# Eight pairs' channel transforms: the low parts of the left operands against the table's high half only

## The chip, the cores and the metric

The kernel runs on one core of a Trainium2 chip. The metric is the device time of one execution in microseconds (us); for the kernel before it is 1575.81 us, the median of three runs (1575.69 to 1577.49). One execution was profiled.

## The reference

Two layers work on a prompt of 2048 positions and a sample of 512, each of width 1024, in float32. Layer 0 is windowed attention. Layer 1, in which the change lies, mixes by a two-dimensional Fourier transform over the positions and over the channels of each of four groups of 256:

```python
def fourier_layer(x, g, w_gate, w_out):
    b, s, d = x.shape
    h = rmsnorm(x, g)
    hg = h.astype(jnp.float32).reshape(b, s, N_FGROUPS, FGROUP_CH)
    f = jnp.fft.fftn(hg, axes=(1, 3), norm="ortho").real
    f = f.reshape(b, s, d).astype(x.dtype)
    gate = h @ w_gate
    return x + (f * jax.nn.silu(gate)) @ w_out

def trunk(x, ...):
    for i in range(DEPTH):
        j = i // N_MIXERS
        if i % N_MIXERS == 0:
            x = attention_layer(x, attn_norm[j], attn_w_in[j], attn_w_out[j], attn_sink[j], rel_bias)
        else:
            x = fourier_layer(x, fourier_norm[j], fourier_w_gate[j], fourier_w_out[j])
    return rmsnorm(x, final_norm)
```

Weights and activations are float32. Both the prompt and the sample go through the same `trunk`.

## The kernel before

**Numbers in two parts.** TensorE (PE) multiplies operands of type F32R, a float32 with fewer bits of mantissa. To come near float32, an operand is split: ScalarE (ACT) copies it into F32R, which gives the high part, and VectorE (DVE) subtracts that from the source, which gives the low part. A product of two split operands is then a sum of products of parts. `matmul3` (line 117 of the kernel) makes three of the four: high by high, high by low, low by high. Each is one load of the left operand (128 partitions by 128 columns) into the array and one matmul that streams the right operand past it, up to 512 columns, into an accumulator in PSUM.

**Stages.** The attention layer takes about the first 1060 us. From there the Fourier layer walks over ten pairs of 128-row tiles of positions: pairs 0 and 1 of the sample, then pairs 2 to 9 of the prompt. For each pair it normalises the two tiles, transposes them on PE (`turn`, line 1089, into PSUM tiles `tr...`), forms sums and differences of them, splits these (`parts`, `odd`, `cross`; lines 1013 and 1015 in `split`, lines 1096 and 1097 in `own`), and uses them twice: as left operands of the gate's products with the weights (`gates`, accumulators W, Z and X, through line 117), and as left operands of the channel transform (`z`, `z_odd_even`). A radix-4 step on DVE (`combine`, lines 1268 and 1277) then joins two pairs, and the results go to DRAM. After about 1300 us the transform over the positions and the output products follow.

**The channel transform.** `z_odd_even(i)` handles tile i of a pair: for each of four channel groups it takes a PSUM bank, and for two left operands (`odd` = 0 and 1) it multiplies by a table of 128 columns for each. The table `ch` holds its high and its low half side by side, so `ch[:, 0, :, odd * P : (odd + 1) * P]` has 2 x 128 = 256 columns. Both parts of the left operand meet both halves, which makes four products of parts in two matmuls of 256 columns (line 1160). The left operands are `S[1]` and `diff` (the trace's names `S` and `tTd`) for tile 1, and `S[4]` and `mixed` (`S` and `tC`) for tile 0. Behind the four matmuls of a group, ACT (line 1167) takes the sums that came from the table's low half out of the bank, and DVE (line 1168) adds those from its high half. The transform of tile 1 runs from hook 5 of the gate products of the pair ahead, that of tile 0 from hook 6. In pairs 0 and 1, those of the sample, tile 0 goes through `z` with `matmul3`; only their tile 1 goes through `z_odd_even`.

**What sets the order.** A planner takes the instructions as the program issues them, keeps dependencies, and sets an order for each engine by its own costs; on the chip each engine then works its list in that order and waits by semaphores. PSUM banks for the transposes and the transforms come from one pool of five, those of W, Z and X from another of three.

Of the kernel before, what the change touches and what calls it, by code (L numbers as in the profile page):

```python
# [19 lines left out]
P = 128  # L20
# [22 lines left out]
def encoder(  # L43
# [22 lines left out]
    odd = dram.tile([3, 2, P, D], F32, name="odd")  # L66
# [9 lines left out]
    def bank(name):  # L76
        if turning:
            return two_banks(name)[:, 0]
        return banks[-1].tile([P, 512], F32, tag="bank", name=name)
# [911 lines left out]
    def fourier_phase(tail):  # L991
        with ExitStack() as es:
# [13 lines left out]
            ch = ready["chan"]  # L1006

            def zt(name):
                return right([P, D], F32, name)
# [58 lines left out]
            class Pair:  # L1068
# [80 lines left out]
                def z_odd_even(self, i=1):  # L1149

                    t = self.ts[i]
                    out_of = (self.S[1], self.diff) if i else (self.S[4], self.mixed)
                    self.zs[i] = zt(f"z{t}")
                    for g in range(4):
                        ps = bank(f"z{t}_{g}")
                        for odd, m in enumerate(out_of):

                            to = ps[:, odd * 256 : odd * 256 + 256].rearrange("p (a n) -> p a n", a=2)
                            for part in range(2):
                                PE.matmul(  # L1160
                                    to, m[part][:, g * P : (g + 1) * P], ch[:, 0, :, odd * P : (odd + 1) * P],
                                    start=part == 0, stop=part == 1,
                                )
                        v = ps.rearrange("p (o a n) -> p a o n", o=2, a=2)
                        out = self.zs[i][:, g * 256 : g * 256 + 256].rearrange("p (n o) -> p o n", o=2)
                        scale = 1.0 if t >= SEQ // P else 0.5
                        ACT.activation(out, v[:, 1], AF.Copy, scale=scale)
                        last_z[0] = DVE.scalar_tensor_tensor(out, v[:, 0], scale, out, ALU.mult, ALU.add)
# [138 lines left out]
            for i, s in enumerate(tail):  # L1307
# [7 lines left out]
                if 1 <= i < 9:  # L1315
                    w, k = split_steps[i - 1]
# [690 lines left out]
```

## Time and profile before

| what | value |
|---|---|
| median of three runs | 1575.81 us (1575.69 to 1577.49) |
| the profiled execution's own time | 1575.53 us |
| its span, first to last instruction | 1573.5 us |
| mean granted TensorE clock | 0.999 |
| DVE busy | 1169.3 us (74%) |
| ACT busy | 884.9 us (56%) |
| POOL busy | 446.3 us (28%) |

The page of the profile gives the busy time of each engine, the span in 40 slices, the chain of work that ended last, and the costliest groups of instructions. PEld is the loading of left operands into the array, which has a lane of its own beside PE. A group's row reads: line, engine, operation, out <- in, the left operand's size (128*128), the size streamed, the count, busy time in us, the mean duration of one in ns, and the idle time before. The duration of a matmul includes the way through the array, so consecutive matmuls overlap: what one costs in a row of many is the distance from one start to the next, which the chain of waits shows (time over count). All F32R operands stand as "f32" in the rows.

### The profile page before, as it was taken

To read this page: it belongs to the slowest core of one execution; us is meant where nothing else is said; L and a number is where in the kernel's file an instruction comes from. 1 tells how busy PE (TensorE), PEld (TensorE's weight loads), DVE (VectorE), ACT (ScalarE), POOL (GpSimd) and SP (SyncE) were. 2 spreads that over 40 slices of the span, in tenths; PEclk is the share of its full clock that TensorE was granted. 3 is DMA by queue.
4 is the path that set the end of the run, shared out by engine and by line. 5 is a ranking of instruction groups with operands and counts; after the bars stand their busy time and mean duration, and the time that the engine had idled before them with its cause. 6 is when DMAs were issued, how large, how long until landed. Compare 5 with 4: busy or idle time off the path is not lost.

```text
span 1573.5 us, 27706 instructions
## 1 busy us (share of the span) xinstructions
PE 1561.3 (99%) x9818; PEld 1308.6 (83%) x9818; DVE 1169.3 (74%) x2841; ACT 884.9 (56%) x2120; POOL 446.3 (28%) x614
## 2 busy tenths in 40 slices
PE   9999999999999999999999999999999999999998
PEld 7888888888898888988888888888888888888886
DVE  5888665877548776377863577768989888989886
ACT  6788535677237774266851567646655564343353
POOL 2575652421403414124223142122121121111100
PEclk9999999999999999999999999999999999999999
DMA  8598695665865576656649665665565569557852
GB/s 290 196 331 292 230 360 208 222 238 201 294 228 197 203 267 234 242 193 237 256 150 330 229 232 195 245 250 205 211 238 199 207 235 409 182 201 285 296 195 94
DMA packets 100998, 373.91 MB, mean 238 GB/s; under 512 B 11267, under 2 KB 22283, under 8 KB 83452
## 3 DMA queue, kind: packets, MB, share of 16 engines
q1 hardware_dynamic: 83148, 298.17, 53.3%
q0 software_dynamic: 16400, 70.04, 11.4%
q10 hardware_dynamic: 1312, 3.94, 0.6%
q8 instruction: 78, 1.28, 0.3%
q14 instruction: 60, 0.49, 0.1%
HBM read 280.84 MB, written 91.26 MB: 236 GB/s over the span
## 4 chain that ended last, share of the span: by engine, by line
PE 89%; DMA 4%; DVE 3%; issue 2%; ACT 1%; POOL 0%; POOLq 0%; ACTq 0%; SPq 0%; DVEq 0%
PE gp L117 14%; PE qp L117 14%; PE spt L117 11%; PE op L117 7%; PE av L615 6%; PE spt L530 6%; PE W L117 5%; PE vp L117 3%; PE fo L117 3%; PE pt L589 3%; PE Wo L117 3%; PE Z L117 3%; PE z L1160 2%; PE Zo L117 2%; PE X L117 1%
## 5 line engine op out<-in xcount | busy, mean ns | idle before, releaser
L117 PE MATMUL gp<-h,wg 128*128 128x512 f32 x960 | 237.6, 396 | 0.0
L117 PE MATMUL qp<-h,wq 128*128 128x512 f32 x960 | 237.0, 396 | 0.0
L549 DVE CUSTOM_DVE_ANT_0 S<-spt,b 128x385 f32<-128x385 f32 (+1 forms) x320 | 156.5, 527 | 105.4 <-PE spt L530 68.3
L117 PEld LDWEIGHTS gp<-h,wg 128*128 128x128 f32 x960 | 174.9, 188 | 37.2 <-issue 1.0
L117 PEld LDWEIGHTS qp<-h,wq 128*128 128x128 f32 x960 | 174.9, 188 | 36.4 <-issue 0.2
L557 ACT ACTIVATE S<-S 128x385 f32<-128x385 f32 (+1 forms) x320 | 188.8, 596 | 19.5 <-DVE S L549 19.3
L597 ACT CAST pts<-pt 128x384 fp32r<-128x384 f32 (+1 forms) x240 | 100.6, 458 | 168.8 <-PE pt L589 160.1
L598 DVE TENSOR_TENSOR pts<-pt,pts 128x384 fp32r<-128x384 f32 (+1 forms) x240 | 114.3, 520 | 23.4 <-ACT pts L597 22.4
L639 POOL TENSOR_TENSOR uT<-o,uT 128x256 fp32r<-128x256 f32 x75 | 55.6, 741 | 229.4 <-ACT uT L638 229.3
L117 PE MATMUL spt<-wo,uT 128*128 128x512 f32 x480 | 120.4, 391 | 0.0
L117 PE MATMUL op<-wo,uT 128*128 128x512 f32 x480 | 118.9, 391 | 0.0
L530 PE MATMUL spt<-kwin,qab 64*128 64x384 f32 (+1 forms) x960 | 118.6, 353 | 0.0
L615 PEld LDWEIGHTS av<-pts,v 128*128 128x128 f32 x576 | 101.4, 188 | 18.8
L117 PE MATMUL fo<-wo,tTu 128*128 128x512 f32 x480 | 115.6, 392 | 0.2 <-ACT wo L1743 0.2
L615 PE MATMUL av<-pts,v 128*128 128x512 f32 (+1 forms) x576 | 115.7, 341 | 0.0
L117 PEld LDWEIGHTS op<-wo,uT 128*128 128x128 f32 x480 | 89.4, 188 | 18.5
L117 PEld LDWEIGHTS spt<-wo,uT 128*128 128x128 f32 x480 | 89.1, 188 | 18.3
L117 PEld LDWEIGHTS fo<-wo,tTu 128*128 128x128 f32 x480 | 88.2, 188 | 17.9 <-ACT wo L1743 0.6
L569 DVE TENSOR_SCALAR S<-S 128x384 f32<-128x384 f32 (+1 forms) x192 | 95.9, 499 | 6.8
L530 PEld LDWEIGHTS spt<-kwin,qab 64*128 64x128 f32 x960 | 74.6, 186 | 28.3 <-issue 25.7
L635 POOL TENSOR_TENSOR o<-o,s 128x256 f32<-128x256 f32 x75 | 55.4, 738 | 134.8 <-DVE o L633 134.5
L589 PEld LDWEIGHTS pt<-ident,S 64*128 64x128 f32 x1328 | 78.2, 138 | 4.5 <-issue 2.1
(337 smaller groups left out, 3210.6 us busy)
## 6 DMA issues: line engine op xcount, KB each, us to landing
wo<-wsd SPq DMA_DIRECT2D x32, 1024.0 KB, 5.7
wq<-wsd SPq DMA_DIRECT2D x31, 1024.0 KB, 7.3
wg<-wsd SPq DMA_DIRECT2D x31, 1024.0 KB, 5.8
x<-x1d SPq DMA_DIRECT2D x40, 512.0 KB, 3.7
b<-b21d SPq DMA_DIRECT2D x40, 512.0 KB, 4.7
b<-rowd SPq DMA_DIRECT2D x40, 384.0 KB, 4.1
xs<-in_x_dram SPq DMA_DIRECT2D x23, 512.0 KB, 7.4
s2d<-gt POOLq DMA_DIRECT2D x40, 256.0 KB, 4.2
```

The costliest lines, as they stand in the source:

```text
L117: ins = pe(PE.matmul(out, a[i], b[j], start=start and i + j == 0, stop=stop and i == 1, skip_group_check=more))
L530: pe(PE.matmul(banks[j][:, 2 + k0 * P : 2 + k1 * P], res["q"][rows, qp, b * P : (b + 1) * P], kwin[g][rows, kp, b * P + k0 * P : b * P + k ...
L549: seq(DVE, DVE.tensor_tensor_reduce(out=s[:, e0:e1], in0=ps[:, 1 + e0 : 1 + e1], in1=st["bias"][:, j, 386 - e1 : 386 - e0][:, ::-1], scale ...
L557: last_exp[0] = seq(ACT, ACT.activation(s[:, e0:e1], s[:, e0:e1], AF.Exp, bias=s[:, 386:387], scale=-1.0, accum_out=s[:, 387:388]))
L569: seq(DVE, DVE.tensor_scalar(s[:, ks], s[:, ks], den, None, ALU.mult))
L589: pe(PE.transpose(ps[h][:, kb, j, :], ss[j][rows, 1 + kb * P : 1 + (kb + 1) * P], ident[rows, rows]))
L597: seq(ACT, ACT.copy(hi, ps[:, k0:k1]))
L598: seq(DVE, DVE.tensor_tensor(lo, ps[:, k0:k1], f32(hi), ALU.subtract))
L615: pe(PE.matmul(to, v, pt, start=n == part == 0, stop=part == 1 and n in (1, len(todo) - 1), skip_group_check=n > 1,))
L635: eng.tensor_tensor(o, o, s, ALU.mult)
L639: low = eng.tensor_tensor(lo, o, f32(hi), ALU.subtract)
L1160: PE.matmul(to, m[part][:, g * P : (g + 1) * P], ch[:, 0, :, odd * P : (odd + 1) * P], start=part == 0, stop=part == 1,)
```

## The change

In `z_odd_even` the second matmul, that of the low part of the left operand (`part` = 1), takes only the high half of the table for the pairs of the prompt (`self.n > 1`): 128 columns in place of 256, and it adds to the first 128 of the 256 sums alone. The product of low part by low half is no longer made. The number of matmuls and of loads stays.

```diff
                             for part in range(2):
+                                w = 1 if part and self.n > 1 else 2
                                 PE.matmul(
-                                    to, m[part][:, g * P : (g + 1) * P], ch[:, 0, :, odd * P : (odd + 1) * P],
+                                    to[:, :w], m[part][:, g * P : (g + 1) * P], ch[:, 0, :w, odd * P : (odd + 1) * P],
                                     start=part == 0, stop=part == 1,
                                 )
```

The planner's order moves at four places on PE, and around them on the other engines. The first place is the transform of tile 0 of pair 2 (left operands S and tC), on PE, where the first product of the next gate (W, left operand tTb) is near. Before:

```order
L1160 MATMUL z_0_13359<-chan_sb,S_2_13269 128x256 x2
L1160 MATMUL z_0_13359<-chan_sb,tC_13300 128x256
L117 MATMUL W_13405<-wB_0_12646,tTb_0_13227 128x512 x2
L1160 MATMUL z_0_13359<-chan_sb,tC_13300 128x256
L117 MATMUL W_13405<-wB_0_12646,tTb_0_13227 128x512
L117 MATMUL W_13405<-wB_1_12664,tTb_0_13227 128x512
L1160 MATMUL z_1_13366<-chan_sb,S_2_13269 128x256 x2
L1160 MATMUL z_1_13366<-chan_sb,tC_13300 128x256 x2
L117 MATMUL W_13405<-wB_1_12664,tTb_0_13227 128x512 x2
L1160 MATMUL z_2_13373<-chan_sb,S_2_13269 128x256 x2
```

Now, from the end of the first group (the rows ahead of these alternate in the same way):

```order
L1161 MATMUL z_0_13359<-chan_sb,tC_13300 128x256
L1161 MATMUL z_0_13359<-chan_sb,tC_13300 128x128
L1161 MATMUL z_1_13366<-chan_sb,S_2_13269 128x256
L1161 MATMUL z_1_13366<-chan_sb,S_2_13269 128x128
L1161 MATMUL z_1_13366<-chan_sb,tC_13300 128x256
L1161 MATMUL z_1_13366<-chan_sb,tC_13300 128x128
L1161 MATMUL z_2_13373<-chan_sb,S_2_13269 128x256
L1161 MATMUL z_2_13373<-chan_sb,S_2_13269 128x128
L1161 MATMUL z_2_13373<-chan_sb,tC_13300 128x256
L1161 MATMUL z_2_13373<-chan_sb,tC_13300 128x128
```

Every second matmul is now 128 columns wide, and the six matmuls of W that stood between those of z now stand behind the last group. The same happens at tile 0 of pairs 4, 6 and 8, where seven matmuls of W move; the order of PE is otherwise as it was.

The second place is DVE just ahead of the same transform: the low part of tC (line 1015) and the addition for the first group of tile 1's transform (z_0_13314). Before:

```order
L1015 TENSOR_TENSOR S_2_13296<-s_2_13242,S_2_13296 128x512
L1243 TENSOR_TENSOR c_13156<-c_13156,X_13155 128x512
L1015 TENSOR_TENSOR tC_13300<-s_2_13242,tC_13300 128x512
L1168 SCALAR_TENSOR_TENSOR z_13313<-z_0_13314,z_13313 128x2x128
L1205 SCALAR_TENSOR_TENSOR gt_0_13309<-gt_0_13309,c_13156 128x512
```

Now:

```order
L1015 TENSOR_TENSOR S_2_13296<-s_2_13242,S_2_13296 128x512
L1244 TENSOR_TENSOR c_13156<-c_13156,X_13155 128x512
L1169 SCALAR_TENSOR_TENSOR z_13313<-z_0_13314,z_13313 128x2x128
L1015 TENSOR_TENSOR tC_13300<-s_2_13242,tC_13300 128x512
L1206 SCALAR_TENSOR_TENSOR gt_0_13309<-gt_0_13309,c_13156 128x512
```

The low part of tC, for which PE's second matmul by tC waits, now stands behind one more operation. The same two operations change places at pairs 4, 6 and 8. On ACT some operations of lines 1167, 1204, 1013 and 1056 change places with a neighbour in the same stretch, on POOL one small operation at three places, and one load of `b` on SP's queue moves ahead of two loads of `wo` near the end of the stretch.

## The prediction

> **What bounds the kernel now.** I read the page's busy times and its chain of waits first, and then the stage of the change by itself.
>
> ```profile
> span 1573.5 us, 27706 instructions
> PE 1561.3 (99%) x9818; PEld 1308.6 (83%) x9818; DVE 1169.3 (74%) x2841; ACT 884.9 (56%) x2120; POOL 446.3 (28%) x614
> PEclk9999999999999999999999999999999999999999
> PE 89%; DMA 4%; DVE 3%; issue 2%; ACT 1%; POOL 0%; POOLq 0%; ACTq 0%; SPq 0%; DVEq 0%
> ```
>
> PE is busy 99% of the span, at the full granted clock in every slice, and 89% of the chain that ended last is PE. The changed pairs run from 1108 to 1300 us; over windows the columns are the window, its length, then busy time (count) of PE, PEld, DVE, ACT and POOL, the granted clock, and the share and rate of the DMA.
>
> ```profile
> 1108.00:1300.00 192.00, 191.41 (x1018) 163.79 (x1017) 173.09 (x290) 115.15 (x234) 36.98 (x61) 1.00 0.61 217
> ```
>
> Of 192.0 us PE idles 0.6. So what a matmul of this stage costs more or less on PE, the kernel gains or loses almost in full; DVE (173.1 us, 90%) is next.
>
> **How many, and at what price now.** The groups by form in that window:
>
> ```profile
> L117 PE MATMUL W<-wT,S 128*128 128x512 f32 x184 | 45.0, 393 | 0.0
> L1160 PE MATMUL z<-chan_sb,S 128*128 128x256 f32 x128 | 25.6, 282 | 0.0
> L1089 PE MATMUL trb<-ident,x 128*128 128x128 f32 x112 | 14.5, 272 | 0.6 <-DVE x L1081 0.6
> L1160 PE MATMUL z<-chan_sb,tC 128*128 128x256 f32 x64 | 13.8, 287 | 0.0
> L1160 PE MATMUL z<-chan_sb,tTd 128*128 128x256 f32 x64 | 12.9, 283 | 0.0
> ```
>
> Line 1160 has 128 + 64 + 64 = 256 matmuls here. Every second one is of a low part: 8 pairs x 2 tiles x 4 groups x 2 operands = 128 change. Durations of about 282 ns overlap; the distance between starts stands in the chain of waits inside the window (start, length, what, count):
>
> ```profile
> 1112.09 1.91 PE z L1160 x16
> 1114.01 2.75 PE W L117 x12
> ...
> 1125.28 0.87 PE trb L1089 x8
> 1126.16 2.74 PE W L117 x12
> ```
>
> 1.91 / 16 = 119 ns for 256 columns, 2.74 / 12 = 228 ns for 512 columns, and 0.87 / 8 = 109 ns for a float32 transpose of 128 columns. From 256 to 512 columns a column costs (228 - 119) / 256 = 0.43 ns; in a transpose it costs 109 / 128 = 0.85 ns.
>
> **Term 1: the 128 narrow matmuls.** No row of this trace has a product of F32R parts under 256 columns. Some of the narrowest products and of the 128-wide transposes of the whole program:
>
> ```profile
> L117 PE MATMUL vp<-wv,h 128*128 128x256 f32 x384 | 50.3, 283 | 0.0
> L530 PE MATMUL spt<-kwin,qab 64*128 64x256 f32 x192 | 20.1, 313 | 0.0
> L117 PE MATMUL ABp<-gp,tbp 128*128 128x256 f32 x96 | 14.3, 281 | 0.0
> L1025 PE MATMUL tru<-ident,us 128*128 128x128 f32 x32 | 4.3, 273 | 0.0
> L222 PE MATMUL spt<-ident,inv 128*128 128x128 f32 x23 | 3.3, 272 | 0.0
> ```
>
> So the price of the new form has to be bounded. Below: the straight line through 512 and 256 columns, continued to 128, gives 119 - 128 x 0.43 = 64 ns. That is 55 ns less, and 128 x 55 = 7.0 us gained. Above: what is read at one column in 0.43 ns is shown for F32R from 256 columns up only; 4-byte data at 128 columns is shown only in transposes, and there a column takes twice as long, though the right operand has the same 4 bytes. If the narrow form loses the fast price of F32R and is computed as full float32, a transpose is the cheapest example of it: with the identity on one side, only one operand has two halves, and it costs 2 column times. With two such operands it is 2 x 2 = 4 column times: 128 x 4 x 0.43 = 218 ns, or, with the fixed part in the row of 512 columns, 228 ns. That is 228 - 119 = 109 ns more for each, and 128 x 109 = 14.0 us lost.
>
> The Trainium skill, page "FP8 and Floating Point Precision", section "TensorE Precision Notes", says that true float32 takes four passes through the array and that reduced precision reads float32 cut shorter. No run here shows a float32 product that isn't a transpose; by that rule, if the narrow form counts as true float32, the loss is the same 14 us.
>
> Between the two ends stands the load of the left operand, one for each matmul, whatever its width. Two windows, the first in the transform, the second in a product of 512 columns, and three groups of loads of the whole program:
>
> ```profile
> 1112.10:1113.70 1.60, 1.60 (x15) 1.60 (x15) 1.60 (x4) 1.37 (x4) 0.00 (x0) 1.00 0.59 172
> 1109.00:1111.40 2.40, 2.40 (x12) 2.01 (x11) 2.40 (x5) 0.83 (x2) 0.00 (x0) 1.00 0.75 288
> ...
> L117 PEld LDWEIGHTS W<-wT,S 128*128 128x128 f32 x240 | 44.2, 188 | 8.8 <-DVE wT L1015 0.2
> L1089 PEld LDWEIGHTS trb<-ident,x 128*128 128x128 f32 x160 | 18.5, 140 | 4.0 <-PE Z L117 1.0 <-DVE xrl L701 0.6 <-issue 0.2
> L1160 PEld LDWEIGHTS z<-chan_sb,tTd 128*128 128x128 f32 x80 | 12.6, 191 | 0.1
> ```
>
> At 256 columns PEld is busy 1.60 of 1.60 us with loads of 191 ns that overlap; at 512 columns it rests. The load already fills the time of a 256-column matmul, so the lower end of 64 ns is hardly to be reached: the narrower matmul would wait for its load. That leaves "no change" and "slower", and of these I take the upper end, 14.0 us: the only 128-wide rows of 4-byte data pay the double price per column, which says that the fast price hangs on the form and is not a property of 4-byte operands.
>
> **Term 2: the moved W products and tC.** At tile 0 of pairs 2, 4, 6 and 8, W no longer fills the time until tC's low part is there. Timeline of the first place, before:
>
> ```profile
> 1116.42 0.68 DVE L1243 TENSOR_TENSOR c<-c,X 128x512 f32<-128x512 f32 x1
> 1116.59 0.40 PE L1160 MATMUL z<-chan_sb,S 128*128 128x256 f32 x2
> 1116.97 0.39 PE L1160 MATMUL z<-chan_sb,tC 128*128 128x256 f32 x1
> 1117.02 0.68 DVE L1015 TENSOR_TENSOR tC<-s,tC 128x512 fp32r<-128x512 f32 x1
> 1117.19 0.63 PE L117 MATMUL W<-wB,tTb 128*128 128x512 f32 x2
> 1117.62 0.41 DVE L1168 SCALAR_TENSOR_TENSOR z<-z,z 128x256 f32<-128x256 f32 x1
> 1117.76 0.39 PE L1160 MATMUL z<-chan_sb,tC 128*128 128x256 f32 x1
> ```
>
> tC's low part is ready at 1117.02 + 0.68 = 1117.70, and one operation of 0.41 us now stands ahead of it: 1118.11. PE reaches the transform later by the eight narrow matmuls of tile 1 (8 x 0.109 = 0.87): 1116.59 + 0.87 = 1117.46, and the matmul by tC's low part three matmuls on (0.12 + 0.23 + 0.12): 1117.93. It waits 0.2 us at each of four places, 0.8 in all; behind it in PE's list stand the rest of z and then W. If the narrow matmuls cost no more than now, it waits 1118.11 - 1116.59 - 3 x 0.12 = 1.2 us, 4.6 us in all.
>
> Against that, a slower PE swallows waits that it has now:
>
> ```profile
> PE trb L1089 <- DVE x L1081: 0.6, 1, 0.6
> PEld z L1160 <- DVE tC L1015: 0.4, 1, 0.4
> PEld z L1160 <- ACT tC L1013: 0.2, 1, 0.2
> ```
>
> These sum to 1.2 us. I set term 2 to zero, with ends of +0.8 and -1.2 in the slow case. The four evacuations of a group and the operations that changed places on ACT, POOL and SP run beside PE and have, if PE is slower, more time than now (ACT 115.2 of 192 us); without that cover each evacuation on DVE would cost its 0.41 us.
>
> **Sum.** 1575.5 (the profiled execution's own time, 0.3 below the median of the runs) + 14.0 + 0 = 1589.5 us. This case's own ends are 128 x (218 - 119) = 12.7, less 1.2, and 128 x (240 - 119) = 15.5, plus 0.8, which gives 1587 to 1592; 240 is two pipelined loads of 119 to 120 for one matmul.
>
> **The rivals.**
>
> *The narrow form pays more still.* If a full float32 product needs its left operand loaded in two halves, and these don't overlap with the stream, a matmul costs up to 2 x 191 = 382 ns: 128 x (382 - 119) = 33.7 us, 1609. Half way, at 300 ns, it is 23.2 us, 1598.7. For it: loads already fill PEld at 256 columns. Against it: loads of 191 ns follow at 119 ns there, so they do overlap.
>
> *It takes as long as before.* The load sets the pace, 119 ns, or two column times as in a transpose, 109 ns: 0 to -1.3 us. For it: PEld without a gap. Against it: it holds only if the fast price of F32R lasts at 128 columns, or a product goes as a transpose. Term 2 then adds up to 4.6 us, less what W's later place gives back; I count 1575 to 1578, the same within what can be told.
>
> *Faster: the stream sets the pace.* One mechanism: PE takes 0.43 ns a column at 128 columns too, and the loads pipeline closer than 119 ns. It decides as soon as a matmul costs less than 119 - 3.2 / 128 x 1000 = 94 ns; at 64 ns it is -7.0 us, 1568.5, and DVE's 173.1 us would still fit into 185. For it: the straight line through two widths. Against it: PEld, which shows no shorter distance. The Trainium skill, page "TensorE: Matmul & The Clock Gate", section "Back-to-back issue gap", gives 81 ns for a load and a matmul of 128 columns and 131 ns at 512; by that it would be 128 x (119 - 81) = 4.9 us faster. The trace does not agree with it for this type: 228 ns at 512.
>
> **How the numbers follow.** About 0.2% (3.2 us) is what a measurement of this kernel can tell from no change. Forecast (1587 to 1592): 0.68. Dearer still (1592 to 1609): 0.15. As long as before: 0.09. Faster: 0.08. So slower 0.83, same 0.09, faster 0.08. The range of 1584 to 1605 holds the forecast, with 3 us below it for waits that I don't see, and most of the dearer case, about 0.8; the two other cases are left out.
>
> **What would show it.** In the profile after, a row of line 1161 with 128x128 x128 in place of half of the 256-wide ones. If I am right, its matmuls last about 390 ns (as the 393 of 512 columns) and not under 282, 16 matmuls of tile 1 take 8 x 0.12 + 8 x 0.23 = 2.8 us in the chain of waits where they take 1.91, and the stage is 206 us long where it is 192. PE stays without gaps at tile 0 of the four pairs but for some 0.2 us each. The prediction is wrong if the narrow matmuls follow one another at 119 ns or less.

## The result and the profile after

The changed kernel takes 1580.95 us (median of 6 runs, 1580.0 to 1582.39) against 1575.06 us before: ratio 1.0034, interval 1.0024 to 1.0044. In a second set on another occasion the ratio was 1.0030 (1.0019 to 1.0041). It is slower by 4 to 6 us; 14 were forecast, and the time lies below the range.

The page of the profile after, the same rows as before:

```profile
span 1577.9 us, 27706 instructions
PE 1562.3 (99%) x9818; PEld 1308.8 (83%) x9818; DVE 1169.2 (74%) x2841; ACT 884.2 (56%) x2120; POOL 442.4 (28%) x614
PE 87%; DVE 6%; DMA 3%; issue 2%; ACT 1%; POOL 0%; SPq 0%; ACTq 0%; POOLq 0%; DVEq 0%
```

The span grew by 4.4 us, while PE's busy time grew by 1.0 and the share of DVE in the chain rose from 3% to 6%. So most of the time isn't in the matmuls. Their groups by form, in a window (1099 to 1310 us) around the changed pairs:

```profile
L1161 PE MATMUL z<-chan_sb,S 128*128 128x256 f32 x64 | 20.7, 323 | 1.1 <-DVE z L1169 1.1
L1161 PE MATMUL z<-chan_sb,S 128*128 128x128 f32 x64 | 14.3, 223 | 0.0
L1161 PE MATMUL z<-chan_sb,tC 128*128 128x256 f32 x32 | 10.9, 341 | 2.6 <-ACT tC L1013 2.5
L1161 PE MATMUL z<-chan_sb,tTd 128*128 128x256 f32 x32 | 10.7, 336 | 0.0
L1161 PE MATMUL z<-chan_sb,tC 128*128 128x128 f32 x32 | 7.6, 236 | 1.6 <-DVE tC L1015 1.6
L1161 PE MATMUL z<-chan_sb,tTd 128*128 128x128 f32 x32 | 7.1, 222 | 0.0
```

The 128-wide matmuls last 222 ns, 60 less than the 282 that a 256-wide one took before, and not 390 as forecast. The end of a matmul is modelled in the profile, its start is not, and the starts say the same: the next matmul starts 0.06 us after a narrow one (timeline).

```profile
1189.38 0.22 PE L1161 MATMUL z<-chan_sb,S 128*128 128x128 f32 x1
1189.44 0.39 PE L1161 MATMUL z<-chan_sb,tTd 128*128 128x256 f32 x2
```

But the 256-wide ones now last 336 ns even where PE waits for no other engine: what one gives, the next takes. A whole transform shows the balance (chain of waits, start, length, what):

```profile
1189.43 1.79 PE z L1161 x16
1191.22 2.81 PE W L117 x12
1194.03 1.79 PE z L1161 x16
1195.82 2.81 PE W L117 x12
```

Before, 16 matmuls took 1.91 us and the twelve of W behind them 2.75; now it is 1.79 and 2.81. Together that is 4.60 where it was 4.66: some 0.07 us for each of 16 transforms, 1.1 us in all, and no more.

The loss stands in the waits of the weight loads between 1100 and 1300 us (us in total, times, longest):

```profile
PEld z L1161 <- ACT tC L1013: 3.1, 4, 1.3
PEld z L1161 <- DVE tC L1015: 2.4, 4, 0.7
PEld z L1161 <- DVE z L1169: 1.7, 4, 0.5
PEld W L117 <- DVE c L1240: 0.9, 3, 0.4
```

8.1 us in all, where the rows before had 0.6 for tC. All but the last stand at tile 0 of pairs 2, 4, 6 and 8, from where the planner had moved W away. The timeline at pair 6, rows of PE, ACT and DVE:

```profile
1218.74 0.34 PE L1161 MATMUL z<-chan_sb,S 128*128 128x256 f32 x2
1219.24 0.60 ACT L1013 CAST tC<-s 128x512 fp32r<-128x512 f32 x1
1219.36 0.42 DVE L1169 SCALAR_TENSOR_TENSOR z<-z,z 128x256 f32<-128x256 f32 x1
1219.88 0.69 DVE L1015 TENSOR_TENSOR tC<-s,tC 128x512 fp32r<-128x512 f32 x1
1219.89 0.39 PE L1161 MATMUL z<-chan_sb,tC 128*128 128x256 f32 x1 [0.81 <-ACT tC L1013]
1220.62 0.33 PE L1161 MATMUL z<-chan_sb,tC 128*128 128x128 f32 x1 [0.34 <-DVE tC L1015]
1221.28 1.08 DVE L1169 SCALAR_TENSOR_TENSOR z<-z,z 128x256 f32<-128x256 f32 x3
1221.76 0.45 PE L1161 MATMUL z<-chan_sb,S 128*128 128x256 f32 x2 [0.34 <-DVE z L1169]
```

PE waits three times in a row: for tC's high part from ACT, for its low part from DVE, and then for a bank of PSUM, which comes free when DVE has taken tile 1's transform out of it. With W between, PE had work there. The same place before:

```profile
1215.58 0.60 ACT L1013 CAST tC<-s 128x512 fp32r<-128x512 f32 x1
1215.90 0.40 PE L1160 MATMUL z<-chan_sb,S 128*128 128x256 f32 x2
1216.23 0.38 PE L1160 MATMUL z<-chan_sb,tC 128*128 128x256 f32 x1
```

The cast that makes tC's high part ended 0.3 us after the start of the transform (1216.18 against 1215.90); now it ends 1.1 us after it (1219.84 against 1218.74).

In this execution the stretch from pair 2's tile 1 (start 1111.93 before, 1110.23 after) to pair 9's tile 0 (1291.05 and 1297.68) is 8.3 us longer. The terms found come to 8.0: 8.1 of waits less the 0.6 of before, plus 1.6 of a stretch in which the clock fell to half (experiment 8), less the 1.1 gained. The span grew by 4.4 alone, since this execution was 1.7 us ahead at the start of the stretch, 1.4 of them since the first 43 us, which the change doesn't touch, and 2.2 us came back behind it, most of them where PE waits for DVE at the transform over the positions. Of the weight loads' waits from 1300 us on, before:

```profile
PEld ABp L117 <- DVE gp L1424: 3.2, 6, 0.7
PEld Bs L117 <- DVE us L1468: 1.0, 1, 1.0
```

and after:

```profile
PEld ABp L117 <- DVE gp L1425: 2.3, 5, 0.7
```

### The profile page after: what moved, and what is told of

It is laid out like the page before. It is cut to its first block, busy times and chain, and to the rows that moved or that the text cites. A ratio compares the mean times of both kernels' runs of the same rounds, so it can differ in the third digit from the quotient of the medians.

```text
span 1577.9 us, 27706 instructions
## 1 busy us (share of the span) xinstructions
PE 1562.3 (99%) x9818; PEld 1308.8 (83%) x9818; DVE 1169.2 (74%) x2841; ACT 884.2 (56%) x2120; POOL 442.4 (28%) x614
## 4 chain that ended last, share of the span: by engine, by line
PE 87%; DVE 6%; DMA 3%; issue 2%; ACT 1%; POOL 0%; SPq 0%; ACTq 0%; POOLq 0%; DVEq 0%
PE gp L117 14%; PE qp L117 14%; PE spt L117 11%; PE op L117 7%; PE av L615 6%; PE spt L530 6%; PE W L117 5%; PE fo L117 5%; PE vp L117 3%; PE pt L589 3%; PE Wo L117 3%; PE Z L117 3%; PE Zo L117 2%; PE X L117 1%; PE z L1161 1%
```

## The experiments

Two theories at the outset: A, the moved order costs the time and the narrow form nothing; B, the narrow matmuls cost it. To tell them apart, the order of the instructions was held by edges that fix only the order on an engine and add no wait, at the end of the program:

```diff
     fourier_phase(attention_phase())
+    held = (
+        [13361, 13362, 13409, 13410, 13363, 13411, 13412, 13367, ...],
+        ...
+    )
+    known = {i.name: i for i in nc.cur_bb.bb.instructions}
+    for row in held:
+        for a, b in zip(row, row[1:]):
+            tc.add_manual_dep(known[f"I-{b}"], f"I-{a}", ISSUE, reason="issue order")
```

Each row lists instructions of one engine in the order wanted. From the Fourier layer's stretch on, the orders named below hold exactly on all five engines.

**1. Narrow matmuls, old order.** The changed kernel with the rows of the kernel before.

> The changed kernel's narrow matmuls, but every engine held to the order that the kernel before has (order edges alone, no waits). Theory A, the moved order costs the time and a narrow matmul costs no more than a wide one: 16 transforms each 0.12 us shorter (1.79 us where 1.91 were, in the two traces), so about 1.9 us faster than before, 1573 us, with no wait for tC beyond that of before. Theory B, the narrow matmuls cost the time: as slow as the changed kernel, 1580 to 1581 us.

Measured: 1574.23 us against 1575.32, ratio 0.9996 (0.9987 to 1.0004). The waits of its weight loads for tC are those of before:

```profile
PEld trb L1089 <- PE Z L117: 2.3, 2, 1.3
PEld z L1161 <- DVE tC L1015: 0.4, 1, 0.4
PEld z L1161 <- ACT tC L1013: 0.3, 1, 0.3
```

B falls: the narrow form costs nothing. Its gain of about a microsecond can't be told from no change here: the interval holds 1.

**2. Wide matmuls, new order.** The kernel before with the rows of the changed one.

> The kernel before with its 256-column matmuls, every engine held to the order of the changed kernel. Theory A: nearly as slow as the changed kernel, 5 to 8 us over before (the waits at tC come back, the 1.9 us of the narrower matmuls are missing), 1580 to 1583 us. Theory B: no slower than before, 1575 us.

Measured: 1579.54 us, ratio 1.0029 (1.0018 to 1.0040), just under the range expected. A holds: the order alone makes the loss. The waits are those of the changed kernel:

```profile
PEld z L1160 <- ACT tC L1013: 3.1, 4, 1.0
PEld z L1160 <- DVE tC L1015: 2.4, 4, 0.7
PEld z L1160 <- DVE z L1168: 1.6, 4, 0.5
PEld W L117 <- DVE c L1239: 0.8, 3, 0.5
```

**3. and 4. Which part of the order.** Narrow matmuls, with PE in the old order and the other engines in the new one, and the reverse.

> The narrow matmuls, PE held to the order of before (W's products again between those of z), the other engines to the order of the changed kernel (tC's low part one operation later on DVE). Theory A1, the missing W products are what lets the waits through: near the kernel before, 1573 to 1576 us. Theory A2, the later tC on ACT and DVE is what PE waits for, and W only hides part of it: 1577 to 1579 us. Theory B: 1580 us.

> The narrow matmuls, PE held to the order of the changed kernel (W behind z), the other engines to the order of before (tC's low part one operation earlier). Theory A1: as slow as the changed kernel less 4 x 0.4 us, 1578 to 1580 us. Theory A2: most of the loss is gone, 1575 to 1577 us. Theory B: 1580 us.

Measured: 1575.5 us (1.0001, 0.9992 to 1.0010) with PE in the old order, 1579.87 us (1.0023, 1.0015 to 1.0032) with PE in the new one. So it is PE's order, W among z or behind it, that decides the time (A1). The other engines' order shows in the waits. With PE in the old order and the rest in the new one, PE still waits for tC's high part, while W covers the rest:

```profile
PEld z L1161 <- ACT tC L1013: 3.5, 4, 1.3
PEld z L1161 <- DVE tC L1015: 0.4, 1, 0.4
```

With PE in the new order and the rest in the old one, that wait is small and the two others are there:

```profile
PEld z L1161 <- DVE tC L1015: 2.1, 4, 0.6
PEld z L1161 <- DVE z L1169: 1.6, 4, 0.4
PEld z L1161 <- ACT tC L1013: 0.8, 2, 0.6
```

So the wait for the high part comes with the other engines' new order, and those for the low part and the bank with PE's. The first is hardly to be seen in the time: 1575.5 us against 1574.23 in experiment 1. In the profile of experiment 3 the stretch from pair 2's tile 1 (1110.37) to pair 9's tile 0 (1292.76) is 3.3 us longer than before, and as in the changed kernel 2.2 us come back behind it. The loss of experiment 4 doesn't look like waits alone: nine of its eleven executions had a mean granted clock of 0.997 or 0.998 and took 1578.1 to 1581.3 us, and the two with 0.999 took 1575.8 and 1575.9. How much of it is the clock's was not separated (experiment 8 has more on this).

**5. and 6. tC earlier.** If tC is what PE waits for, making it sooner should help. At the four places, the cast of tC goes ahead of the square of the next tile on ACT, and its low part directly behind that of S on DVE, once with PE in the new order and once with all else in the old one.

```diff
 DVE, at pair 2
  L1015 S_2_13296
+ L1015 tC_13300
  L1244 c_13156
  L1169 z_13313<-z_0_13314
- L1015 tC_13300
```

> The changed kernel, its PE order kept (W behind z), but at the four places tC's high part stands one operation earlier on ACT (ahead of the square of the next tile) and its low part two operations earlier on DVE. If what PE waits for is tC, and the moved W only uncovers that wait, the 8 us of waits in the stage shrink by half or more: 1574 to 1577 us. If the order of W costs by itself (bank or weight load), it stays at 1579 to 1581 us.

> The narrow matmuls in the order of the kernel before, with tC earlier in the same way. If the theory of waits is right, there is little left to gain here, 0.3 us at each of four places, set against a later square of the next tile: 1572 to 1575 us, the best of all, or equal to the kernel before.

Measured: 1583.81 us (1.0052, 1.0038 to 1.0066) in the new order, against 1574.19 us (0.9997, 0.9988 to 1.0006) in the old one. The first is a clear miss: not better but slower than the changed kernel (1578.98 us on the same occasion). Its waits:

```profile
PEld z L1161 <- DVE z L1169: 6.4, 8, 0.9
PEld z L1161 <- DVE tC L1015: 1.7, 4, 0.5
```

The wait for ACT is gone, but the wait for a bank grew from 1.7 to 6.4 us: the first of DVE's additions that free the banks now stands behind tC. The waits sum to 8.5 us with 0.4 at W, about as many as the 8.1 of the changed kernel. So tC alone is not what is short. DVE has both to do, tC's low part and the additions of tile 1, before PE can go through tile 0, and in each order of DVE's list that was tried PE lacked other work meanwhile. That this version is slower than the changed one is explained in part: its profile has a stretch at half the granted clock, worth 1.6 us, which that of the changed kernel on the same occasion hasn't (experiment 8), and it was 2.0 us behind that one already at the start of the stretch (1111.97 against 1110.02). Nor does the planner's swap of the two operations on DVE, which the prediction booked as a loss, matter much: behind PE's new order the waits for the low part and the bank are 2.1 and 1.6 us without it (experiment 4) and 2.4 and 1.7 with it.

**7. What sets the pace.** All the prompt's transform matmuls narrow, in the old order; high by high and low by high go into the two halves of the bank. This version leaves out the product of the high part with the table's low half.

```diff
-                                w = 1 if part and self.n > 1 else 2
+                                w = slice(part, part + 1) if self.n > 1 else slice(0, 2)
                                 PE.matmul(
-                                    to[:, :w], m[part][:, g * P : (g + 1) * P], ch[:, 0, :w, odd * P : (odd + 1) * P],
-                                    start=part == 0, stop=part == 1,
+                                    to[:, w], m[part][:, g * P : (g + 1) * P],
+                                    ch[:, 0, 0:1 if self.n > 1 else 2, odd * P : (odd + 1) * P],
+                                    start=part == 0 or self.n > 1, stop=part == 1 or self.n > 1,
                                 )
```

> All 256 matmuls of the prompt's transforms 128 columns wide (high by high and low by high, into the two halves of the bank; the product of the high part with the table's low half is left out), in the order of the kernel before. If the load of the left operand sets the pace (108 to 116 ns from load to load), 16 matmuls still take 1.74 to 1.8 us and the time is that of the narrow kernel in the old order, 1573 to 1575 us. If the stream sets it (60 ns after a narrow matmul), 16 take 0.96 us and the time falls by about 13 us, to 1562. If a narrow matmul were priced as full float32 (228 ns), it would rise by 28 us.

Measured: 1573.42 us, ratio 0.9988 (0.9979 to 0.9997). A transform in the chain of waits:

```profile
1187.33 1.74 PE z L1161 x16
1189.07 2.85 PE W L117 x12
```

and a window inside one (columns as before):

```profile
1111.50:1112.90 1.40, 1.40 (x15) 1.40 (x14) 1.40 (x3) 0.89 (x3) 0.00 (x0) 1.00 0.37 73
```

A third fewer columns than in the changed kernel, and 1.74 us in place of 1.79: 1.74 / 16 = 109 ns for a matmul of 128 columns, with PEld busy 1.40 of 1.40 us. The load of the left operand sets the pace. The matmuls of this version last 266 to 275 ns on average, which fits that each of them waits for its load. Two column times, the price of a transpose, would give 109 ns too; against that stand the 0.06 us from a narrow matmul to the next start in the changed kernel. The Trainium skill, page "TensorE: Matmul & The Clock Gate", section "LDWEIGHTS (loading the stationary operand)", gives the number of columns divided by 1.2 for a load, an estimate of 107 ns at 128. The pace of 109 ns agrees with it; the durations of these loads in the rows, 190 to 192 ns, do not.

**8. The changed kernel again.**

> The changed kernel unaltered, on the same chip as the three others: 1580 to 1582 us. Its profile shows whether the stretch of half the granted clock behind the waits at pair 4 (3.4 us at 427 ns for 512 columns) comes again; if it hangs on the phase of the waits it will stand at another of the four places, or be missing.

Measured: 1578.98 us, 1.0030 (1.0019 to 1.0041), somewhat under the expectation. In the first profile of the changed kernel, twelve matmuls of W behind the waits at pair 4 began like this (timeline, then window):

```profile
1169.45 4.10 PE L117 MATMUL W<-wB,tTb 128*128 128x512 f32 x10
...
1169.50:1172.80 3.30, 3.30 (x10) 2.65 (x9) 2.56 (x7) 1.64 (x4) 1.10 (x2) 0.50 1.01 318
```

and in this one:

```profile
1169.50:1172.80 3.30, 3.30 (x17) 2.73 (x17) 2.56 (x7) 1.98 (x5) 1.10 (x2) 1.00 0.94 307
```

In the first the granted clock is 0.50, and ten matmuls pass where 17 pass at full clock: 7 x 0.228 = 1.6 us. In the second it does not happen, with the same waits ahead of it. It did happen in two other kernels with W behind the transform, at pair 8, in experiment 4 and in experiment 5:

```profile
1269.80:1273.10 3.30, 3.30 (x12) 3.01 (x13) 2.58 (x8) 1.85 (x4) 1.22 (x3) 0.50 0.89 308
1275.80:1279.10 3.30, 3.30 (x10) 2.54 (x9) 2.55 (x7) 1.43 (x4) 1.10 (x2) 0.50 0.98 308
```

So it came in three of the five profiles with PE's new order, each time behind or among waits at tile 0, and in this part of the program in none of the seven with another order. The mean clock of the executions agrees: it is 0.998 or less in 25 of 36 with PE's new order, the first set and experiments 2, 4, 5 and 8, and in 8 of 142 with another, the kernel before among them. The fall goes with PE's new order, then, and is most likely a second cost of its waits. It isn't the whole loss: with a mean clock of 0.999, four executions of experiment 8 took 1578.4 to 1580.4 us and five of experiment 2 took 1578.3 to 1580.8, some 4 us over the kernel before.

**9. and 10. W ahead of the transform.** On PE, all twelve matmuls of W's first product stand ahead of tile 0's transform at the four places; the rest is in the old order. Once with narrow matmuls, once with wide ones.

```diff
 PE, at pair 2
+ L117 W_13405, all twelve
  L1161 z_0_13359<-S
  L1161 z_0_13359<-tC, high part
- L117 W_13405, two
  L1161 z_0_13359<-tC, low part
- L117 W_13405, two
...
```

> The narrow matmuls; the other engines in the order of the kernel before; on PE all twelve matmuls of W's first product stand ahead of tile 0's transform at the four places (in the changed kernel they stand behind it, in the kernel before some stand inside). If the loss is that PE has nothing to do while DVE frees banks and makes tC, 2.7 us of W ahead of the transform cover all of it: no wait for tC or for a bank there, 1572 to 1574.5 us, not slower than before. If any place but the old one costs, 1577 us or more.

> The same order of PE with the 256-column matmuls of the kernel before. It tells what the order gives without the change: 1573 to 1575.5 us, 1.1 us above the narrow one (16 transforms x 0.07 us).

Measured: 1572.68 us (0.9988, 0.9979 to 0.9997) narrow, 1573.91 us (0.9996, 0.9987 to 1.0005) wide. The only wait that the view lists for the narrow kernel's weight loads between 1100 and 1300 us:

```profile
PEld trb L1089 <- PE Z L117: 1.1, 1, 1.1
```

No wait for tC and none for a bank is left. This version beats the kernel before by 2.1 us and, going by the ratios, the changed one by some 7. Its difference from the wide one, 1.2 us, fits the 1.1 counted in the trace for the change itself, but the two intervals overlap. Both steps are near the limit of what can be told; for the narrow one the interval lies just below 1.

## Why the prediction was wrong

- **What bounds the kernel** was right: a PE without gaps, where a lost microsecond is lost in the end, less what later waits give back.
- **Term 1 failed.** The step that failed is the choice of the upper bound for the narrow matmul, 228 ns as full float32, argued from the price per column of a transpose. Measured: 222 ns long, 60 ns shorter than a wide one of before, which is 60 / 128 = 0.47 ns a column, near the 0.43 between 256 and 512. The fast price holds at 128 columns, 128 x 109 ns of loss did not exist, and the transpose was the wrong neighbour.
- **The lower bound was seen and rightly closed.** PEld without a gap at 256 columns meant that the load sets the pace; 109 ns (experiment 7) against 119 leaves almost nothing to gain. Had this row been weighed alone, the term would have been 0 to -1.3 us; it is -1.1.
- **Term 2 failed in its size and its mechanism.** I set it to zero, and at most 4.6 us if the narrow matmuls cost nothing. The weight loads wait 8.1 us: the wait for tC's low part, the only one in the estimate, is 2.4 of it. Left out were the wait for the high part on ACT, 3.1, and that for a bank, 1.7. The operations that changed places on ACT and the four evacuations were priced as running beside PE with time to spare; but the cast of tC came 0.8 us later against the transform at pair 6, and it is the other engines' new order that brings this wait (experiments 3 and 4). The fall of the clock behind the waits, 1.6 us in the first profile, stood in no term.
- **The sign was right for the wrong reason.** The rival "it takes as long as before" had the mechanism, the load's pace plus the waits that W no longer covers, but was given 0.09, and its 1575 to 1578 us fell short of the measured 1579 to 1581. That the forecast said slower, and the kernel is slower, was luck: the cost that it was built on did not exist. The dearer and the faster rival are both excluded by experiments 1 and 7.
- **The waits to be swallowed** (1.2 us) did not matter, since PE did not become slower.
- **The signs to look for** worked: narrow rows under 282 ns and 16 matmuls in less than 1.91 us told at once that term 1 was wrong.

## What to carry to other kernels

Before pricing fewer columns, look at whether the weight load has a gap beside such a matmul; if it has none, a narrower stream buys nothing. An edit that changes one instruction's size can change a planner's order in places that the diff doesn't show, and there the cost may lie: list what was filling the waits, price every wait that it covered, the banks' release included, and look at the granted clock behind them. Holding the order fixed separates the two in two runs.

## What the runs showed of the hardware

- A product of F32R parts keeps about its price per column at 128 columns (222 ns long against 282 at 256, the next start 0.06 us later). With one load for each matmul it is paced by that load, at 109 ns (experiment 7); in pairs of 256 and 128 columns the pace is 112 (1.79 / 16).
- The granted clock can fall to one half for at least 3.3 us behind waits of under a microsecond each: at pair 4 in one profile of the changed kernel and not in the other, with PE's rows for the waits alike, and at pair 8 in experiments 4 and 5. The Trainium skill, page "TensorE: Matmul & The Clock Gate", Part 1, puts the drop after an idle window of about 3.4 us; no wait of PE in this part of the changed kernel was over 1.1 us, so here a single wait of that length was not needed, and the measurement decides. What decides whether it falls was not tried.
